# The last quarter of the MLP's down projections computed as seven half-size block products, with some additions done by accumulating DMAs

## The chip, the cores and the metric

The kernel runs on one core of a Trainium2 chip. The metric is the device time of one execution in microseconds (us); lower is better. A core has a matrix engine (TensorE, PE in the profile), three elementwise engines (VectorE or DVE, ScalarE or ACT, GpSimd or POOL), a queue engine that issues transfers (SyncE or SP) and 16 DMA engines. Each engine works through its own instructions in order and waits on semaphores for the others. POOL can issue transfers too, and those may add to what stands at their destination ("accumulating").

## What is computed

Two decoder layers on 512 tokens of width 1024, all in float32. The part that matters here is the MLP of each layer and what follows it:

```python
for i in range(DEPTH):                       # DEPTH = 2
    ...                                      # attention, added to h
    hn = rmsnorm(h, norm_mlp_g[i])
    u = jnp.square(jax.nn.relu(hn @ w_mlp_up[i]))      # 512 x 4096
    h = h + u @ w_mlp_down[i]                          # 512 x 1024
    gate = jax.nn.sigmoid(rmsnorm(h, norm_ple_g[i]) @ w_ple_gate[i])
    h = h + (p[i] @ w_ple_proj[i]) * gate
return rmsnorm(h, final_norm_g)
```

## The kernel before

Activations are held transposed: `h` is eight tiles h0 to h7 of 128 features by 512 tokens. For float32 accuracy each operand is split into a rounded high part and a low part (`hi`/`lo`, `wh`/`wl`, `uh`/`ul`), and each product is three matmuls: high by high, high by low, low by high (`mm3`, L137 to L142). ACT makes the high part with a copy, DVE (in the MLP) the low part with a subtraction, so every piece of weights passes ACT, then DVE, then PE.

The MLP's 4096 hidden features are worked in four chunks `ch` of 1024, each of four blocks `c`. `up(ch, c)` multiplies a block of 256 hidden features into two PSUM banks, and DVE and ACT apply the relu, the scale and the square (L720, L721); L732 and L733 split the result into `uh` and `ul`. `down(ch, c)` multiplies the chunk's hidden features by the weights of output columns 256c to 256c+255, that is h[2c] and h[2c+1].

For the first three chunks, `down` uses a Strassen-Winograd scheme: the product of 2 x 2 blocks from seven block products instead of eight. `up` makes four combinations of the hidden blocks (T1 to T4, L724 to L728), so its split covers 1792 columns; `down` makes four weight sums on DVE (L742 to L745) and takes seven products of 12 matmuls with 256 columns each. Two products go straight into `h` (L784, L786); the four side products are gathered over the chunks in `sides[c]` (L771), and `side_sums(c)`, eight DVE operations on 256 columns, adds them to `h` at the end.

The last chunk (ch = 3) is done in the ordinary way: `down_last(c)` runs 2 x 24 matmuls of 512 columns, DVE adds each bank to `h` (L804), and `nxt.done(k)` prepares the next norm: ACT scales and splits h[k] (L182), DVE makes the low part (L183), ACT squares h[k] (L241), and DVE adds the squares up (L247). Its `up` needs no T blocks and splits 1024 columns.

The order of instructions on each engine is set when the kernel is built, by a scheduler that goes by its own estimate of times; the program text gives dependences and a starting order. Weights come in 1 MB transfers on SP's queue into two buffers named `raw`; the hidden tile `u` and the tile `sums` have one buffer each. In both layers the last chunk is followed by the gate projection, which needs h0 to h7; in layer 1 (`ple_final`) PE first transposes `h` (L858).

Of the kernel before, what the change touches and what calls it, by code (L numbers as in the profile page):

```python
# [12 lines left out]
F32 = mybir.dt.float32  # L13
# [6 lines left out]
P = 128  # L20
D = 1024
S = 512
# [40 lines left out]
def trunk(  # L63
# [8 lines left out]
    def nm(s):  # L72
        uid[0] += 1
        return f"{s}_{uid[0]}"
# [155 lines left out]
    class Norm:  # L230
# [3 lines left out]
        def done(self, k, stats=True):  # L234
            self.hl[k] = split_tile(h[k], gcol(self.kind, self.layer, k))
            if stats:
                self.stats(k)

        def stats(self, k, after=()):
            sq = t2k("e" if self.acc else "rstd")  # L240
            act = nc.scalar.activation(sq, h[k], AF.Square)  # L241
# [460 lines left out]
    def mlp(layer, fpool, norm, nxt):  # L702
# [6 lines left out]
        def up(ch, c):  # L709
# [12 lines left out]
            parts = slice(0, 7)  # L722
            if ch < NCH - 1:
                nc.vector.tensor_tensor(  # L724
                    u[:, T1:T3 + 1:2], u[:, B11:B22 + 1:3], u[:, T3:T3 + 1].to_broadcast([P, 2, HW]), op=ALU.subtract)
                nc.vector.scalar_tensor_tensor(
                    u[:, T2], u[:, T1], -1.0, u[:, B22], op0=ALU.mult, op1=ALU.subtract)
                nc.vector.scalar_tensor_tensor(  # L728
                    u[:, T4], u[:, T2], -1.0, u[:, B21], op0=ALU.mult, op1=ALU.subtract)
            else:  # L730
                parts = slice(B11, B22 + 1)
            nc.scalar.activation(uh[:, parts], u[:, parts], AF.Copy)  # L732
            nc.vector.tensor_tensor(ul[:, parts], u[:, parts], uh[:, parts].bitcast(F32), op=ALU.subtract)  # L733
            hidden[ch, c] = (uh, ul)

        def down(ch, c):
            raw = wload(w_down[layer, 4 * ch + c])
            rv = raw.rearrange("p (s k c) -> p s (k c)", s=4, k=4)
            A12, A22, S3, A11 = range(4)
            sums = fpool.tile([P, 3, S], F32, tag="sums", name=nm("sums"), bufs=1)  # L740
            S1, S2, S4 = range(3)
            nc.vector.tensor_tensor(sums[:, S1], rv[:, S3], rv[:, A22], op=ALU.add)  # L742
            nc.vector.tensor_tensor(sums[:, S2], sums[:, S1], rv[:, A11], op=ALU.add)
            nc.vector.tensor_tensor(rv[:, S3], rv[:, S3], rv[:, A11], op=ALU.add)
            nc.vector.tensor_tensor(sums[:, S4], sums[:, S2], rv[:, A12], op=ALU.add)  # L745

            def split(src):
                n = src.shape[1]
# [4 lines left out]
                src = src.rearrange("p s (k c) -> p s k c", k=4)  # L753
                nc.scalar.activation(hi, src, AF.Copy)  # L754
                nc.vector.tensor_tensor(lo, src, hi.bitcast(F32), op=ALU.subtract)
                return hi, lo
# [9 lines left out]

            def total(x, bank):
                if ch == 0:
                    nc.scalar.activation(sides[c][x], banks[bank], AF.Copy)
                else:  # L770
                    nc.vector.tensor_tensor(sides[c][x], sides[c][x], banks[bank], op=ALU.add)  # L771

            w = split(sums[:, S1:S2 + 1])
# [10 lines left out]
            nc.vector.tensor_tensor(h[2 * c], h[2 * c], banks[2], op=ALU.add)  # L784
            product(3, 0, w, 1, T4, True, True)
            nc.vector.tensor_tensor(h[2 * c + 1][:, 0:HW], h[2 * c + 1][:, 0:HW], banks[3][:, 0:HW], op=ALU.subtract)  # L786
# [10 lines left out]
        def down_last(c):  # L797
            blk = block(w_down[layer, 4 * (NCH - 1) + c], KT, P)
            uhl = [tuple(x[:, B11 + 2 * i:B11 + 2 * i + 2].rearrange("p a c -> p (a c)") for x in hidden[NCH - 1, k])
                   for k in range(4) for i in range(2)]  # L800
            for i in range(2):
                acc = ps_wide()
                lin(acc, blk[i][0], blk[i][1], uhl, 0, KT)
                nc.vector.tensor_tensor(h[2 * c + i], h[2 * c + i], acc, op=ALU.add)  # L804
                nxt.done(2 * c + i)

        for c in range(4):
            up(0, c)
        for ch in range(1, NCH):
            up(ch, 0)  # L810
            for c in range(4):
                down(ch - 1, c)
            for c in range(1, 4):
                up(ch, c)
                if ch == NCH - 1:
                    side_sums(c)
        side_sums(0)
        for c in range(4):
            down_last(c)
# [145 lines left out]
def _feeds(a):  # L965
# [3 lines left out]
    for layer, w in enumerate((a["w_in_even"][0], a["w_in_odd"][0])):  # L969
        blocks = []  # L970
        for j, g in enumerate(GROUPS[layer]):
# [4 lines left out]
            else:  # L976
# [20 lines left out]
        "w_down": np.array([[_pack(down[l], range(8 * ch, 8 * ch + 8), 256 * c, 256, 2) if ch == 3 else  # L997
                             _pack4(down[l], 8 * ch, 256 * c) for ch in range(4) for c in range(4)] for l in layers]),
# [31 lines left out]
```

## Time and profile before

| What | us |
|---|---|
| Median of three timed runs | 1310.36 (1309.34 to 1310.42) |
| The profiled execution, its time | 1308.87 |
| Its span, from first to last instruction | 1307.1 |
| Matmul records busy | 1283.7 |
| VectorE busy | 973.5 |
| ScalarE busy | 686.0 |
| GpSimd busy | 189.8 |

The profile is of one execution of 1308.87 us; 1.8 us of it lie outside the span. Busy times of different engines overlap, so they don't add up to the span. PE has matmul records in 98% of the span; a record's end is modelled and reaches over the start of the next one, so what a matmul costs is read from the distance between starts. GpSimd's busy time lies in the attention parts, where it makes low parts of weights.

### The profile page before, as it was taken

The page shows a single profiled execution, that of the slowest core. Times are in us where ns is not written, and L with a number is a line of the kernel's source. Part 1 is how long each engine was busy: PE and PEld are TensorE (multiplying, and loading weights), DVE is VectorE, ACT ScalarE, POOL GpSimd, SP SyncE. Part 2 cuts the span into 40 slices and gives each one's busy share as a digit, 9 for nine tenths or more (in the row PEclk, how much of TensorE's full clock was granted, in tenths as well). Part 3 has the DMA queues.
Part 4 walks back from the last instruction along what each step waited for, and adds up shares of the span by engine and source line. Part 5 has one row for each costly group of instructions (what it writes and reads, how often), then busy time and mean ns, then how long its engine had stood idle before and what let it go on. Part 6 is the DMA issues. An engine that isn't in the chain of part 4 may idle for free.

```text
span 1307.1 us, 18561 instructions
## 1 busy us (share of the span) xinstructions
PE 1283.7 (98%) x7256; PEld 1117.4 (85%) x7256; DVE 973.5 (74%) x1623; ACT 686.0 (52%) x1117; POOL 189.8 (15%) x160
## 2 busy tenths in 40 slices
PE   9999999999999999999999999999999999999997
PEld 7988787888998989988889888788899898998876
DVE  7788888778848869845767877887784885994566
ACT  6666768554535334333456666765553443533344
POOL 2433434410000000000024333222000000000001
PEclk9999999999999999999999999999999999999999
DMA  6421423223232322323432222212223123232241
GB/s 217 135 81 50 140 93 115 89 82 112 86 108 97 102 92 97 129 97 101 157 112 96 84 89 78 69 57 95 99 97 124 70 97 129 73 122 97 97 145 65
DMA packets 28040, 133.20 MB, mean 102 GB/s; under 512 B 3312, under 2 KB 4048, under 8 KB 15280
## 3 DMA queue, kind: packets, MB, share of 16 engines
q1 hardware_dynamic: 27952, 132.01, 29.5%
q8 instruction: 57, 0.93, 0.3%
q14 instruction: 31, 0.25, 0.1%
HBM read 125.63 MB, written 6.37 MB: 101 GB/s over the span
## 4 chain that ended last, share of the span: by engine, by line
PE 85%; DVE 8%; ACT 4%; issue 1%; DMA 1%; SPq 0%; POOL 0%; ACTq 0%; DVEq 0%; POOLq 0%
PE mm L138 10%; PE mm L141 10%; PE mm L142 10%; PE sc L141 6%; PE sc L142 6%; PE sc L138 6%; PE pv L142 5%; PE pv L141 5%; PE pv L138 5%; PE tp L141 5%; PE tp L142 5%; PE tp L138 5%; PE pv L551 2%; PE tp L532 2%; PE sc L506 1%
## 5 line engine op out<-in xcount | busy, mean ns | idle before, releaser
L122 ACT ACTIVATE wh<-raw 128x1024 fp32r<-128x1024 f32 (+1 forms) x168 | 173.4, 1036 | 226.9 <-PE mm L141 63.0
L126 POOL TENSOR_TENSOR wl<-raw,wh 128x512 fp32r<-128x512 f32 (+1 forms) x132 | 177.1, 1364 | 309.3 <-ACT wh L122 303.6
L138 PE MATMUL mm<-hi,wh 128*128 128x512 f32 x472 | 187.0, 396 | 0.6 <-DVE v L443 0.4
L142 PE MATMUL mm<-hi,wl 128*128 128x512 f32 x472 | 184.8, 392 | 0.1
L141 PE MATMUL mm<-lo,wh 128*128 128x512 f32 x472 | 184.6, 391 | 0.0
L128 DVE TENSOR_TENSOR wl<-raw,wh 128x1024 fp32r<-128x1024 f32 x102 | 124.5, 1224 | 41.3 <-ACT wh L122 34.8
L142 PEld LDWEIGHTS mm<-hi,wl 128*128 128x128 f32 x472 | 88.6, 188 | 20.1 <-POOL wl L126 0.5
L138 PEld LDWEIGHTS mm<-hi,wh 128*128 128x128 f32 x472 | 88.7, 188 | 17.3 <-DVE v L443 0.6
L141 PEld LDWEIGHTS mm<-lo,wh 128*128 128x128 f32 x472 | 88.7, 188 | 15.6
L526 ACT ACTIVATE e<-e,mn 128x128 f32<-128x128 f32 (+3 forms) x96 | 53.8, 561 | 65.4 <-DVE mn L523 65.0
L754 ACT ACTIVATE wh<-raw 128x1024 fp32r<-128x1024 f32 x48 | 50.7, 1057 | 69.6 <-PE tp L141 35.1
L733 DVE TENSOR_TENSOR ul<-u,uh 128x1792 fp32r<-128x1792 f32 (+1 forms) x32 | 58.4, 1824 | 23.4 <-ACT uh L732 23.4
L732 ACT ACTIVATE uh<-u 128x1792 fp32r<-128x1792 f32 (+1 forms) x32 | 49.4, 1544 | 48.9 <-DVE u L728 48.7
L138 PE MATMUL sc<-hi,wh 128*128 128x512 f32 x184 | 71.9, 391 | 0.9 <-ACT hi L182 0.9
L141 PE MATMUL sc<-lo,wh 128*128 128x512 f32 x184 | 72.1, 392 | 0.3 <-DVE lo L183 0.3
L142 PE MATMUL sc<-hi,wl 128*128 128x512 f32 x184 | 71.8, 390 | 0.0
L721 ACT ACTIVATE u<-u 128x512 f32<-128x512 f32 x64 | 39.4, 625 | 53.8 <-DVE u L720 53.8
L142 PE MATMUL pv<-uh,wl 128*128 128x256 f32 (+1 forms) x224 | 67.4, 301 | 0.0
L142 PE MATMUL sc<-uh,wl 128*128 128x256 f32 (+1 forms) x224 | 67.3, 301 | 0.0
L141 PE MATMUL pv<-ul,wh 128*128 128x256 f32 (+1 forms) x224 | 67.2, 300 | 0.0
L141 PE MATMUL sc<-ul,wh 128*128 128x256 f32 (+1 forms) x224 | 67.2, 300 | 0.0
L138 PE MATMUL pv<-uh,wh 128*128 128x256 f32 (+1 forms) x224 | 66.6, 297 | 0.0
(259 smaller groups left out, 3645.4 us busy)
## 6 DMA issues: line engine op xcount, KB each, us to landing
raw<-in_w_up_dram SPq DMA_DIRECT2D x32, 1024.0 KB, 4.9
raw<-in_w_down_dram SPq DMA_DIRECT2D x32, 1024.0 KB, 4.9
raw<-in_w_in_dram SPq DMA_DIRECT2D x23, 1024.0 KB, 4.9
raw<-in_w_gate_dram SPq DMA_DIRECT2D x8, 1024.0 KB, 5.0
bias<-urow SPq DMA_DIRECT2D x24, 256.0 KB, 3.9
raw<-in_w_outa_dram SPq DMA_DIRECT2D x8, 768.0 KB, 4.2
pj<-pjd SPq DMA_DIRECT2D x16, 256.0 KB, 5.0
h<-in_xT_dram SPq DMA_DIRECT2D x8, 256.0 KB, 5.6
```

The lines of the kernel that those rows point to most:

```text
L122: nc.scalar.activation(hi, src, AF.Copy)
L126: nc.gpsimd.tensor_tensor(lo[:, kx], src[:, kx], hi[:, kx].bitcast(F32), op=ALU.subtract)
L128: nc.vector.tensor_tensor(lo, src, hi.bitcast(F32), op=ALU.subtract)
L138: mm = nc.tensor.matmul(acc, lh, rh, start=start, stop=False)
L141: nc.tensor.matmul(acc, lh, rl, start=False, stop=False)
L142: nc.tensor.matmul(acc, ll, rh, start=False, stop=stop)
L526: nc.scalar.activation(e[:, 0:n], e[:, 0:n], AF.Exp, scale=-1.0, bias=mn, accum_out=s)
L532: nc.tensor.transpose(tp[:, j * P:(j + 1) * P], e[:, j * P:(j + 1) * P], ident)
L721: nc.scalar.activation(ui, ui, AF.Square, scale=0.5)
L732: nc.scalar.activation(uh[:, parts], u[:, parts], AF.Copy)
L733: nc.vector.tensor_tensor(ul[:, parts], u[:, parts], uh[:, parts].bitcast(F32), op=ALU.subtract)
L754: nc.scalar.activation(hi, src, AF.Copy)
```

## The change

The last chunk's down projections use the seven products as well, and part of the additions moves from DVE to accumulating DMAs that POOL issues:

- `up` makes the T blocks for every chunk, and its split always covers 1792 columns.
- `down(3, c)` forms two of its weight sums by DMA: the weights' block S3 is loaded into a tile `s1` (two buffers) by SP, block A22 is accumulated onto it by POOL, and block A11 is accumulated onto S3 in `raw`. DVE still makes two sums.
- For c = 0 to 2 the four PSUM banks are collected by `collect`: ACT copies a bank to a staging tile (tag `u`, one buffer), and POOL issues a DMA that adds it to `sides[c][x]`, h[2c] or h[2c+1].
- `finished(c - 1)`, called in `down(3, c)` for c = 1 to 3, runs `side_sums` and `done` for the two `h` tiles of the column before; the squares are added by accumulating DMAs.
- For c = 3 DVE adds straight from PSUM (`combine`).
- The weights of the last chunk are laid out in HBM as those of the others.

```diff
-        def done(self, k, stats=True):
+        def done(self, k, stats=True, dma=False):
...
+            elif dma:
+                nc.gpsimd.dma_start(self.acc, sq, accum_op=ALU.add)
             else:
                 nc.vector.tensor_tensor(self.acc, self.acc, sq, op=ALU.add)
...
-            parts = slice(0, 7)
-            if ch < NCH - 1:
...
-            nc.scalar.activation(uh[:, parts], u[:, parts], AF.Copy)
+            nc.scalar.activation(uh, u, AF.Copy)
...
+            if last:
+                blocks = [src[:, S * x:S * x + S] for x in range(4)]
+                nc.sync.dma_start(s1[:, 0], blocks[S3])
+                nc.gpsimd.dma_start(s1[:, 0], blocks[A22], accum_op=ALU.add)
+                nc.gpsimd.dma_start(rv[:, S3], blocks[A11], accum_op=ALU.add)
+            else:
+                nc.vector.tensor_tensor(s1[:, 0], rv[:, S3], rv[:, A22], op=ALU.add)
+                nc.vector.tensor_tensor(rv[:, S3], rv[:, S3], rv[:, A11], op=ALU.add)
...
+            if last and c < 3:
+                stage = [fpool.tile([P, 7 * HW], F32, tag="u", name=nm("u"), bufs=1), 0]
+
+            def collect(dst, src, sign=1.0):
+                t = stage[0][:, stage[1]:stage[1] + src.shape[-1]]
+                stage[1] += src.shape[-1]
+                nc.scalar.activation(t, src, AF.Copy, scale=sign)
+                nc.gpsimd.dma_start(dst, t, accum_op=ALU.add)
...
+            if last and c:
+                finished(c - 1)
+            if last and c == 3:
+                combine(c, banks[:2], t2k("e"))
...
+        def combine(c, banks, t):
+            left, right = slice(0, HW), slice(HW, S)
+            (s1t1, s2t2), (s3t3, a11b11) = ((x[:, left], x[:, right]) for x in banks)
+            h11, h12, h21, h22 = (h[2 * c + i][:, x] for i in range(2) for x in (left, right))
+            a, x = t[:, left], t[:, right]
+            nc.scalar.activation(a, a11b11, AF.Copy)
+            for dst, y, z, op in ((h11, h11, a, ALU.add), (x, a, s2t2, ALU.add), (h12, h12, x, ALU.add), (h12, h12, s1t1, ALU.add),
+                                  (x, x, s3t3, ALU.add), (h21, h21, x, ALU.subtract), (x, x, s1t1, ALU.add),
+                                  (h22, h22, x, ALU.subtract)):
+                nc.vector.tensor_tensor(dst, y, z, op=op)
+
+        def finished(c):
+            side_sums(c)
+            for i in range(2):
+                nxt.done(2 * c + i, dma=True)
...
-        def down_last(c):
...
-        side_sums(0)
+        side_sums(3)
         for c in range(4):
-            down_last(c)
+            down(NCH - 1, c)
```

Three places show what stands where now (layer 0; layer 1 has the same rows with other numbers).

On ACT, around the second column (c = 1). Before, a column is four operations for each of its two tiles: a weight split (L122), then the scaled split and the square of the h tile just finished.

```order
L122 ACTIVATE wh_1001_5795<-raw_1000_5793 128x1024
L182 ACTIVATE hi_984_5710<-h1_95,gcols_102 128x512
L241 ACTIVATE e_986_5714<-h1_95 128x512
L122 ACTIVATE wh_1003_5799<-raw_1000_5793 128x1024
L182 ACTIVATE hi_993_5753<-h2_96,gcols_102 128x512
L241 ACTIVATE e_995_5757<-h2_96 128x512
```

Now, from the last copy of column 0 (into the staging tile u_993) to the split of column 1's weight sum S4 (e_1020); u_1009 is column 1's staging tile, in the same memory as u_993.

```order
L784 ACTIVATE u_993_5679<-sc_992_5678 128x256
L765 ACTIVATE wh_1022_5903<-raw_1002_5790 128x1024
L765 ACTIVATE wh_1032_5949<-s1_1026_5938 128x512
L784 ACTIVATE u_1009_5803<-tp_1005_5799 128x512
L182 ACTIVATE hi_1014_5874<-h0_94,gcols_102 128x512
L784 ACTIVATE u_1009_5803<-tp_1006_5800 128x512
L241 ACTIVATE rstd_1016_5878<-h0_94 128x512
L182 ACTIVATE hi_1017_5880<-h1_95,gcols_102 128x512
L241 ACTIVATE e_1019_5884<-h1_95 128x512
L765 ACTIVATE e_1020_5887<-sums_1003_5792 128x512
```

The split of S4 now stands behind a copy into u_1009, which has to wait until all four DMAs of column 0 have read u_993, and behind the operations on h0 and h1.

On POOL, at the same place; side_634, side_635, h0 and h1 are the destinations of column 0's collects, s1_1048 is the weight sum of column 3. Before, POOL has no instruction here.

```order
L747 DMA raw_1024_5935<-in_w_down_dram 128x512
L785 DMA side_634_3068<-u_993_5679 128x512
L785 DMA side_635_3069<-u_993_5679 128x512
L746 DMA s1_1048_6084<-in_w_down_dram 128x512
L785 DMA h0_94<-u_993_5679 128x512
L785 DMA h1_95<-u_993_5679 128x256
L785 DMA side_636_3070<-u_1009_5803 128x512
```

The accumulate for column 3's weights was put between column 0's collects, ahead of those into h0 and h1.

On PE, where the last chunk begins. Before, its first matmuls run through two halves of each of the four hidden blocks, and the newest, uh_972, is met after 18 matmuls (one row in three is shown, the high-by-high one):

```order
L138 MATMUL mm_979_5652<-uh_886_4935,wh_975_5644 128x512
...
L138 MATMUL mm_979_5652<-uh_952_5464,wh_975_5644 128x512
...
L138 MATMUL mm_979_5652<-uh_962_5541,wh_975_5644 128x512
...
L138 MATMUL mm_979_5652<-uh_972_5618,wh_975_5644 128x512
```

Now the three older blocks are run into each of four banks (36 matmuls, the last of which is the first row here), then come four matmuls with the newest, uh_984, and then its low part ul_985:

```order
L142 MATMUL sc_992_5678<-uh_974_5575,wl_1001_5759 128x256
L138 MATMUL mm_989_5675<-uh_984_5647,wh_994_5680 128x256
L138 MATMUL mm_990_5676<-uh_984_5647,wh_996_5712 128x256
L138 MATMUL sc_991_5677<-uh_984_5647,e_998_5742 128x256
L138 MATMUL sc_992_5678<-uh_984_5647,wh_1000_5758 128x256
L141 MATMUL mm_989_5675<-ul_985_5648,wh_994_5680 128x256
```

The newest block is met after 36 matmuls of 256 columns instead of 18 of 512, and its split is 1792 columns wide instead of 1024.

More of the change, by code (lines that the diff above doesn't have):

```diff
@@ L741, in down @@
[L741 to L744, printed above, removed]
+            sums = fpool.tile([P, 2, S], F32, tag="sums", name=nm("sums"), bufs=1)
+            s1 = fpool.tile([P, 1, S], F32, tag="s1", name=nm("s1"), bufs=2)
+            S2, S4 = range(2)
+            last = ch == NCH - 1
@@ L745, in down, with split @@
             nc.vector.tensor_tensor(sums[:, S4], sums[:, S2], rv[:, A12], op=ALU.add)
[L747 to L748 removed]
+            def split(*srcs):
+                n = sum(x.shape[1] for x in srcs)
                 if n == 2:
@@ L769, in total @@
                     nc.scalar.activation(sides[c][x], banks[bank], AF.Copy)
-                else:
+                elif not last:
                     nc.vector.tensor_tensor(sides[c][x], sides[c][x], banks[bank], op=ALU.add)
-            w = split(sums[:, S1:S2 + 1])
+                elif c < 3:
+                    collect(sides[c][x], banks[bank])
+            w = split(s1, sums[:, S2:S2 + 1])
             product(0, 0, w, 0, T1, True, False)
```

62 lines of the change are left out of this document (32 added, 30 removed).

## The prediction

> **What bounds the kernel now.** I read the page's busy times and chain first, then the stretches of the two last chunks, then the rows in them.
>
> ```profile
> span 1307.1 us, 18561 instructions
> PE 1283.7 (98%) x7256; PEld 1117.4 (85%) x7256; DVE 973.5 (74%) x1623; ACT 686.0 (52%) x1117; POOL 189.8 (15%) x160
> PE 85%; DVE 8%; ACT 4%; issue 1%; DMA 1%; SPq 0%; POOL 0%; ACTq 0%; DVEq 0%; POOLq 0%
> ```
>
> PE ends 85% of the chain. The table of stretches shows the last chunk of layer 0, then that of layer 1 (length, then busy time of each engine):
>
> ```profile
> 577.00:623.00 46.00, 46.00 (x200) 37.08 (x199) 25.82 (x32) 18.08 (x25) 0.00 (x0) 1.00 0.33 109
> 1205.00:1250.00 45.00, 44.94 (x200) 35.87 (x198) 23.29 (x32) 16.57 (x24) 0.00 (x0) 1.00 0.25 84
> ```
>
> Here PE has no gap at all and the clock is full, while DVE is busy 25.82 us of 46, ACT 18.08 and POOL not once. So in this place each matmul saved is time saved, as long as weights and hidden blocks go on arriving before PE asks for them. The question is whether they do.
>
> **What the products save.** The rows of PE give the first matmul of column 0 and the first matmul behind that column in a chunk that already has seven products; the rows of DVE give one bank of two neighbouring columns of the last chunk.
>
> ```profile
> 333.31 0.28 PE L138 MATMUL sc<-uh,wh 128*128 128x256 f32 x1
> 343.39 0.28 PE L138 MATMUL pv<-uh,wh 128*128 128x256 f32 x1
> 591.06 0.69 DVE L804 TENSOR_TENSOR h<-h,sc 128x512 f32<-128x512 f32 x1 [2.25 <-PE sc L142]
> 602.26 0.69 DVE L804 TENSOR_TENSOR h<-h,tp 128x512 f32<-128x512 f32 x1 [2.20 <-PE tp L142]
> ```
>
> 84 matmuls of 256 columns take 10.08 us, 0.120 each; 48 of 512 columns take 11.20 us, 0.233 each. So the seventh less of arithmetic is worth 1.12 us a column, not 1.4: for four columns in two layers **-9.0 us**. That is the whole gain, and only if nothing makes PE wait.
>
> **Term A: the newest hidden block.** The end of the last up projection before the change, and prices of the wide form from the chunks that have it:
>
> ```profile
> 574.27 0.69 DVE L720 SCALAR_TENSOR_TENSOR u<-pv,rstd 128x512 f32<-128x512 f32 x1 [3.35 <-PE pv L142]
> 575.01 0.62 ACT L721 ACTIVATE u<-u 128x512 f32<-128x512 f32 x1
> 576.76 1.23 DVE L733 TENSOR_TENSOR ul<-u,uh 128x1024 fp32r<-128x1024 f32 x1 [0.39 <-ACT uh L732]
> L724 DVE TENSOR_TENSOR u<-u 128x512 f32<-128x512 f32 x24 | 16.5, 686 | 1.4 <-ACT u L721 1.4
> L726 DVE SCALAR_TENSOR_TENSOR u<-u x24: 416/424/427, 298.5 to 1121.2; 128x256 f32<-128x256 f32 x24
> L732 ACT ACTIVATE uh<-u 128x1792 fp32r<-128x1792 f32 x24 | 40.9, 1704 | 48.7 <-DVE u L728 48.7
> L733 DVE TENSOR_TENSOR ul<-u,uh 128x1792 fp32r<-128x1792 f32 x24 | 48.6, 2024 | 19.8 <-ACT uh L732 19.8
> ```
>
> Now the low part is ready at 577.99, 3.7 us after 574.27, and 18 x 0.233 = 4.2 us of older work cover it. After the change the chain is L720 0.69, L721 0.62, one weight split that DVE has in between (1.22) up to about 2.1 us, then 0.69, twice 0.42 with 0.1 between dependent steps, 1.70 and 2.02: about 7.5 us from the same point, 7.8 from PE's last up matmul. The cover is 36 + 4 matmuls of 0.120 = 4.8. PE waits **3.0 us in each layer**. In earlier chunks `down` comes one `up` later, which hides this; here nothing is left to put in front.
>
> **Term B: the copies, the DMAs and the split of S4.** The trace has no accumulating DMA and none issued by POOL. The nearest rows:
>
> ```profile
> bias<-urow SPq DMA_DIRECT2D x24, 256.0 KB, 3.9
> h<-in_xT_dram SPq DMA_DIRECT2D x8, 256.0 KB, 5.6
> out_dram<-ht SPq DMA_DIRECT2D x8, 256.0 KB, 2.1
> raw<-in_w_down_dram SPq DMA_DIRECT2D x32, 1024.0 KB, 4.9
> 581.98 0.33 SPq L114 DMA_DIRECT2D raw<-in_w_down_dram  x1
> L126 POOL TENSOR_TENSOR wl<-raw,wh 128x512 fp32r<-128x512 f32 x100 | 140.9, 1430 | 235.1 <-ACT wh L122 229.4 <-PE pv L622 5.7
> L769 ACT ACTIVATE side<-sc x8: 577/580/597, 339.1 to 988.2; 128x512 f32<-128x512 f32 x8
> L182 ACT ACTIVATE hi<-h,gcols 128x512 fp32r<-128x512 f32 x48 | 33.5, 713 | 19.8 <-DVE h L804 8.7 <-DVE h L688 7.6 <-DMA h<-in_xT_dram 3.4
> L241 ACT ACTIVATE e<-h 128x512 f32<-128x512 f32 x42 | 25.4, 617 | 4.3 <-DVE h L845 4.3
> L754 ACT ACTIVATE e<-sums 128x512 fp32r<-128x512 f32 x24 | 15.0, 624 | 3.6 <-DVE sums L745 3.6
> L795 DVE TENSOR_TENSOR h<-h,side 128x256 f32<-128x256 f32 x40 | 16.1, 421 | 0.1
> ```
>
> An issue is bounded by 0.33 us (SP's) and 1.43 us (POOL's own work on a tile of this size); I take the middle, 0.9. From issue to landing the same 256 KB takes 2.1 (a store), 3.9 (a load) or 5.6 us (eight loads queued); I take the load, with POOL's 0.9 in place of SP's 0.33: **4.5 us**, 4.1 for half a tile. An accumulate also reads its destination, which speaks against the lower end. The Trainium skill (DMA: Bandwidth & Descriptors, section "Anatomy of one DMA") fits about 2.0 us plus bytes over 436 GB/s for a DMA issued by GpSimd, an estimate of 2.6 us here; by it the sum below would come to about +12 us instead of +24. The 1 MB loads land in 4.9 us where that fit gives 4.4, so the fit is near for plain transfers, but no run here shows an accumulating one.
>
> Count from the end of column 0's last matmul. SP may load column 3's `s1` only after column 1's split has read the buffer, 2.2 us earlier; it lands 3.8 us later, at +1.6. On POOL that accumulate stands ahead of the collects into h0 and h1, so h1's begins at 1.6 + 2 x 0.9 = +3.4 and lands at +7.5. Until then ACT is stuck at its copy into the staging tile, which has one buffer. Behind it stand seven operations, 0.58 + 0.71 + 0.58 + 0.62 + 0.71 + 0.62 + 0.62 = 4.4 us, some 3.9 since neighbours overlap by 0.08, with 0.5 more for the `side_sums` steps that the operations on h wait for. The split of S4 ends at +12.0. PE has 60 matmuls to run meanwhile (column 1's four side products and half a product of column 2), 7.2 us. It waits **4.8 us**.
>
> **Term C: column 2, and what DVE holds back.** The same chain for column 2: the last copy of column 1 is done at +1.5, POOL is free, h3 lands at +5.6, ACT's 4.0 us follow, 9.7 in all. PE has 48 matmuls (5.8 us) and 1.2 us of the next wait: **2.8 us**. That other wait: DVE's step on column 1's sides stands ahead of the low part of column 2's S2, and the side collect, copied by ACT only after the staging tile is free, lands late; S2 is ready 1.2 us after PE wants it, and the same for column 3: **2.4 us**.
>
> **Term D: the last column.** In layer 0 PE has 19 matmuls of the gate projection to run ahead of column 3's S4, 4.3 us, and waits some **1.2 us**. In layer 1 the transposes need h itself, so there is no such cover: **4.5 us**, and `combine` with its eight dependent steps of 0.42 and two splits, where DVE also has to copy the transposes, makes the end about **0.9 us** longer.
>
> What costs nothing: the T blocks of the other three `up` of the chunk (2.4 us more of ACT and DVE, beside 10.9 us of matmuls), and the sums and `side_sums` that move, since DVE is idle for nearly half this stretch. DVE's saved work is worth nothing for that reason too.
>
> **The sum.** Layer 0: 3.0 + 4.8 + 2.8 + 2.4 + 1.2 = 14.2; layer 1: 3.0 + 4.8 + 2.8 + 2.4 + 4.5 + 0.9 = 18.4. Together 32.6 - 9.0 = +23.6. On the profiled execution's 1308.87 us (span 1307.1 and 1.8 around it; the median of the timed runs is 1.5 us higher) that is **1332 us**.
>
> **Rivals.**
> - *The DMAs land early.* At 2.1 us, the store's row, DMAs no longer set B to D; what is left is the order on ACT and DVE: A 3.0, then about 2.3 and 2.0 for columns 1 and 2, 3.3 and 0.9 in layer 1's end, 18.8 - 9.0 less rounding: +10, about 1319 us. For it: these DMAs have the queue nearly to themselves (DMA share 0.33). Against it: an accumulate reads, adds and writes.
> - *The DMAs land late.* From about 5 us on, each accumulated sum of squares, which waits for the one before it, holds POOL's queue in front of the next collects, and the weight sums are late too. Each further us then costs some 14: at 5.6 us +38, 1347 us; at 6, 1351.
> - *The other side: the waits are covered and the products pay.* The mechanism would be a shorter way from column c's last copy to column c + 1's S4. It decides at 7.2 us, PE's own work in between. Then only A remains, 6.0 - 9.0: about 1306 us, and 1300 if A is covered as well. For it: DVE and ACT are half idle. Against it: from the copies to S4 nine ACT operations follow each other in order, with `side_sums` between, which alone is longer than 7.2 us even with DMAs that cost nothing.
> - *It does not do what it says*: the order of instructions shows 84 narrow matmuls a column in the last chunk, so this has no chance worth a number.
>
> **How the numbers follow.** Forecast (DMAs of 3 to 5.2 us) 0.72; early 0.12; late 0.12; covered 0.04, of which I give 0.01 to a result within 0.2% (about what a measurement of this kernel can tell from no change). All but the last are slower by more than 0.2%: slower 0.96, same 0.01, faster 0.03. The range takes in both ends of the DMA's price, 1317 to 1350; only part of the late case and the covered one lie outside.
>
> **What the profile would show.** PE's rows 0.120 apart in the last chunk (the -9.0); a PE gap near 3 us just behind the last up projection that ends on uh and ul (A); gaps of 2 to 5 us once a column that end on ACT's split of `sums` (B, C, D), with ACT idle before its copy into `u` until a DMA landed; from 3 to 5 us to landing for the accumulates and about 0.9 of POOL for each. I am wrong if PE has no gaps there, or if an accumulate lands in under 2 or over 6 us.

## The result, and the profile after

| What | Before | After |
|---|---|---|
| Median of four timed runs, us | 1309.85 (1308.74 to 1310.42) | 1364.28 (1362.95 to 1365.29) |
| The profiled execution, its time and span, us | 1308.87, 1307.1 | 1365.29, 1363.5 |
| Ratio after / before | | 1.0416, 95% interval 1.0400 to 1.0433 |

The kernel became 54.4 us slower. The forecast was 1332 us, 23.6 above the profiled execution, with a range up to 1350: the direction was right, and the loss more than twice as large.

The page of the changed kernel, first the span and the busy times, then the granted TensorE clock in 40 slices:

```profile
span 1363.5 us, 19508 instructions
PE 1294.8 (95%) x7544; PEld 1143.1 (84%) x7544; DVE 1014.7 (74%) x1705; ACT 719.9 (53%) x1191; POOL 233.3 (17%) x210
PEclk9999999999999999978999999999999999998899
```

PE's share fell from 98% to 95% although it has 288 instructions more, and the clock row has dips it did not have. The table of stretches (length, busy time of PE, PEld, DVE, ACT and POOL, granted clock, DMA share) shows the two last chunks, where before PE had no gap and a clock of 1.00:

```profile
600.00:632.00 32.00, 23.88 (x153) 23.68 (x154) 19.28 (x33) 16.54 (x26) 10.41 (x12) 0.73 0.64 123
1262.00:1280.00 18.00, 13.64 (x93) 13.43 (x93) 10.37 (x18) 8.18 (x14) 4.33 (x6) 0.78 0.73 152
```

PE is busy three quarters of the time and, while busy, has the clock only at 0.73 and 0.78. So there are two losses here, waits and a slow clock. The rows of PE that follow a wait (start, duration, what it works on, and in brackets the idle time and what ended it), first layer 0, then layer 1:

```profile
579.87 0.39 PE L138 MATMUL mm<-uh,wh 128*128 128x256 f32 x1 [1.18 <-ACT uh L730]
581.93 0.39 PE L141 MATMUL mm<-ul,wh 128*128 128x256 f32 x1 [1.32 <-DVE ul L731]
604.29 0.58 PE L138 MATMUL pv<-uh,e 128*128 128x256 f32 x1 [8.12 <-ACT e L765]
621.06 0.58 PE L138 MATMUL sc<-uh,e 128*128 128x256 f32 x1 [3.83 <-ACT e L765]
638.18 0.50 PE L142 MATMUL mm<-hi,wl 128*128 128x512 f32 x1 [2.01 <-DVE wl L128]
654.09 0.50 PE L141 MATMUL mm<-lo,wh 128*128 128x512 f32 x1 [4.24 <-DVE lo L183]
...
1237.82 0.39 PE L141 MATMUL mm<-ul,wh 128*128 128x256 f32 x1 [1.32 <-DVE ul L731]
1261.29 0.58 PE L138 MATMUL pv<-uh,e 128*128 128x256 f32 x1 [9.35 <-ACT e L765]
1277.79 0.58 PE L138 MATMUL sc<-uh,e 128*128 128x256 f32 x1 [4.36 <-ACT e L765]
1295.49 0.58 PE L138 MATMUL pv<-uh,e 128*128 128x256 f32 x1 [6.68 <-ACT e L765]
```

The places are those that the prediction named: the newest hidden block (A), the split of S4 in columns 1, 2 and 3 (B, C, D). The time lost at each is 0.16 us more than the bracket, because a record's end lies that much past the place where the next start would have stood. The second loss is seen between the waits. These are starts in column 1 of layer 0, behind the wait of 8.12 us:

```profile
604.88 0.41 PE L138 MATMUL pv<-uh,wh 128*128 128x256 f32 x1
605.10 0.41 PE L141 MATMUL pv<-ul,wh 128*128 128x256 f32 x1
605.31 0.41 PE L142 MATMUL pv<-uh,wl 128*128 128x256 f32 x1
...
610.47 0.28 PE L142 MATMUL pv<-uh,wl 128*128 128x256 f32 x1
610.59 0.28 PE L138 MATMUL pv<-uh,wh 128*128 128x256 f32 x1
610.71 0.28 PE L141 MATMUL pv<-ul,wh 128*128 128x256 f32 x1
```

For some 6 us the matmuls start 0.213 us apart, then 0.120 again. The granted clock there is 0.50 (604.30 to 610.00 us), and this document calls the time lost "half clock". PE's records have no gaps in it, so a search for waits passes over it.

**A ledger of the two losses.** In the two last chunks and what follows them (540 to 665 us and 1190 us to the end) I added up, for each kernel, the time lost in waits of over 0.3 us, and, between neighbouring matmuls without a wait, what their starts stand further apart than 0.120 us (256 columns) or 0.233 us (512). Before has 2.5 us of waits and 1.6 of half clock, and the products save 9.0; so waits + half clock - 13.1 should be the difference in time:

| Kernel | Waits | Half clock | Sum - 13.1 | Measured against before |
|---|---|---|---|---|
| after (profiled execution) | 49.7 | 17.5 | +54.1 | +55.4 |
| collection by VectorE | 18.9 | 9.3 | +15.1 | +15.2 |
| weight sums by VectorE | 38.9 | 15.1 | +40.9 | +40.1 |
| squares by VectorE | 52.4 | 15.8 | +55.1 | +55.8 |
| column 2's squares by VectorE | 47.4 | 16.3 | +50.6 | +50.3 |
| load after collection | 45.9 | 16.9 | +49.7 | +50.0 |
| finishing later | 41.2 | 12.0 | +40.1 | +39.9 |
| a staging tile per column | 50.2 | 15.6 | +52.7 | +50.0 |
| 268 extra matmuls (32.2 us) | 20.5 | 10.8 | +50.4 | +50.2 |
| 329 extra matmuls (39.5 us) | 13.9 | 4.3 | +44.6 | +43.1 |
| no accumulating DMA | 21.5 | 10.4 | +18.8 | +18.9 |
| splits ahead, GpSimd adds | 16.1 | 10.1 | +13.1 | +15.0 |
| splits ahead, VectorE adds | 14.0 | 11.4 | +12.3 | +12.5 |

(The extra matmuls' time, 0.120 us each, is in the sum of their rows; the first row sets the 1365.29 us of the profiled execution against before's median.) Thirteen kernels agree with it within 3 us, nine of them within 1. So the 9.0 us that the products save is there in all of them, and waits and half clock are the whole loss. The ledger only says where the time went; why PE waited is for the experiments. Each of the experiments below is one timed execution beside one of before on the same chip; since executions of one kernel lie up to 2.3 us apart, differences under 3 us are not read.

### The profile page after: what moved, and what is told of

Its sections match the earlier page's. It is cut to its first block, busy times and chain, and to the rows that moved or that the text cites. A ratio compares the mean times of both kernels' runs of the same rounds, so it can differ in the third digit from the quotient of the medians.

```text
span 1363.5 us, 19508 instructions
## 1 busy us (share of the span) xinstructions
PE 1294.8 (95%) x7544; PEld 1143.1 (84%) x7544; DVE 1014.7 (74%) x1705; ACT 719.9 (53%) x1191; POOL 233.3 (17%) x210
## 5 line engine op out<-in xcount | busy, mean ns | idle before, releaser
L122 ACT ACTIVATE wh<-raw 128x1024 fp32r<-128x1024 f32 (+1 forms) x152 | 156.4, 1033 | 162.5 <-PE mm L141 44.4
L128 DVE TENSOR_TENSOR wl<-raw,wh 128x1024 fp32r<-128x1024 f32 x86 | 104.8, 1223 | 32.2 <-ACT wh L122 32.2
L765 ACT ACTIVATE wh<-raw 128x1024 fp32r<-128x1024 f32 x64 | 67.7, 1057 | 67.0 <-PE tp L141 34.9
L746 POOL DMA_DIRECT2D s<-in_w_down_dram x8 | 7.4, 921 | 526.4 <-DVE s L749 506.2
L766 DVE TENSOR_TENSOR wl<-raw,wh 128x1024 fp32r<-128x1024 f32 x64 | 78.2, 1223 | 24.0 <-ACT wh L765 24.0
L731 DVE TENSOR_TENSOR ul<-u,uh 128x1792 fp32r<-128x1792 f32 x32 | 64.8, 2024 | 25.9 <-ACT uh L730 25.9
L730 ACT ACTIVATE uh<-u 128x1792 fp32r<-128x1792 f32 x32 | 54.5, 1703 | 55.3 <-DVE u L728 55.3
L142 PE MATMUL pv<-uh,wl 128*128 128x256 f32 x224 | 64.7, 289 | 0.0
L141 PE MATMUL pv<-ul,wh 128*128 128x256 f32 x224 | 64.6, 289 | 0.0
L142 PE MATMUL sc<-uh,wl 128*128 128x256 f32 x224 | 64.6, 289 | 0.0
```

The costliest lines, as they stand in the source:

```text
L141: nc.tensor.matmul(acc, lh, rl, start=False, stop=False)
L142: nc.tensor.matmul(acc, ll, rh, start=False, stop=stop)
L730: nc.scalar.activation(uh, u, AF.Copy)
L731: nc.vector.tensor_tensor(ul, u, uh.bitcast(F32), op=ALU.subtract)
L765: nc.scalar.activation(hi[:, y], x, AF.Copy)
L766: nc.vector.tensor_tensor(lo[:, y], x, hi[:, y].bitcast(F32), op=ALU.subtract)
```

## Experiments

**Collection.** The banks of columns 0 to 2 are added by VectorE again:

```diff
-                elif not last:
+                elif not (last and c == 3):
                     nc.vector.tensor_tensor(sides[c][x], sides[c][x], banks[bank], op=ALU.add)
-                elif c < 3:
-                    collect(sides[c][x], banks[bank])
...
-            if last and c < 3:
-                collect(h[2 * c], banks[2])
-            else:
-                nc.vector.tensor_tensor(h[2 * c], h[2 * c], banks[2], op=ALU.add)
+            nc.vector.tensor_tensor(h[2 * c], h[2 * c], banks[2], op=ALU.add)
```

> The weight sums and the squares of the last chunk stay on accumulating DMAs; the banks of columns 0 to 2 are added into the side sums and hidden-state tiles by VectorE again, so no staging copy and no collecting DMA is left. Theory (the loss is ScalarE and VectorE standing behind the collecting DMAs, and the half clock that follows TensorE's long waits): no wait over 3.4 us is left before column 1's or column 2's third product, the granted clock stays at 1.00 through the last chunk, and the time is 1316 to 1324 us. Rival, that the weight sums' DMAs are what is late: the time stays above 1350. Rival, that narrow 256-column products do not pay even without waits: 1324 to 1335 with no wait over 1.5 us.

Measured: 1324.87 us, 15.2 over before. PE's rows at the third product of column 1 in layer 0 and of column 3 in layer 1:

```profile
597.12 0.39 PE L138 MATMUL pv<-uh,e 128*128 128x256 f32 x1 [1.27 <-ACT e L765]
1255.51 0.39 PE L138 MATMUL pv<-uh,e 128*128 128x256 f32 x1 [2.04 <-ACT e L765]
```

The long waits are gone, and 39 of the 54 us with them. The clock was not at 1.00 throughout, though: 9.3 us of half clock are left, behind A's two short waits and behind waits of 1 and 2 us. Collection is the main loss; the time came 0.9 us above the theory's range for that remainder. By its time alone the run would fit the rival of narrow products, but that asked for no wait over 1.5 us, and column 3 in layer 1 waits 2.04; the ledger has the products' gain in full.

**Weight sums.** VectorE forms the two sums in the last chunk too:

```diff
-            if last:
+            if False:
                 blocks = [src[:, S * x:S * x + S] for x in range(4)]
```

> Only the weight sums go back to VectorE; collection and squares stay on accumulating DMAs. Theory: the collecting DMAs still hold ScalarE and VectorE, so at least half of the loss stays: 1340 to 1362 us, with waits of 3 us and more before products of the last chunk. Rival, that the weight sums' accumulating DMAs are what is late: 1325 us or less.

Measured: 1349.73 us. As the theory had it, most of the loss stays, but 14.6 us went, though no wait of PE had ended on one of these DMAs. What they did is shown by the next run's rows.

**The load beside the collection.** Column 3's weights are loaded only when column 0's collection has landed:

```diff
-            raw = wload(src)
+            raw = wload(src, landed.get(c, ()) if ch == NCH - 1 else ())
...
-                nc.gpsimd.dma_start(dst, t, accum_op=ALU.add)
+                ad = nc.gpsimd.dma_start(dst, t, accum_op=ALU.add)
+                if c == 0:
+                    landed[3] = [ad.ins]
```

> Nothing is computed differently: the 1 MB load of column 3's down weights waits until the last collecting DMA of column 0 (the 128x256 one) has landed. Theory (that DMA takes 9 to 10 us because the load shares the DMA engines with it): it lands 3.5 to 5 us after its issue, the wait before column 1's third product falls from 8.3 and 9.5 us to 4.5 to 6 us, and the time falls by 5 to 10 us to 1354 to 1359. Rival, that an accumulating DMA behind two others on GpSimd is slow by itself: 9 to 10 us to landing as before, and 1362 us or more.

Measured: 1359.68 us, 0.7 above the theory's range; the waits fell to 5.99 and 6.05 us. First the place after, in the timeline of ScalarE, GpSimd and SyncE's queue:

```profile
591.77 0.63 ACT L765 ACTIVATE wh<-s 128x512 fp32r<-128x512 f32 x1 [1.18 <-PE tp L141]
600.21 0.60 ACT L784 ACTIVATE u<-tp 128x512 f32<-128x512 f32 x1 [7.80 <-DMA h<-u]
603.62 0.61 ACT L765 ACTIVATE e<-sums 128x512 fp32r<-128x512 f32 x1
590.19 2.16 POOL L785 DMA_DIRECT2D h<-u  x2
591.88 0.33 SPq L114 DMA_DIRECT2D raw<-in_w_down_dram  x1
```

ScalarE stands at its copy into the staging tile from 592.4 to 600.2, until the collection into h1 lands; the split of S4 (603.62) stands behind it. While GpSimd still issues h1's DMA, the second of the two, SyncE issues 1 MB of weights. Now the DMA issues between 583 and 603 us (queue, count, size, us from issue to landing), after:

```profile
raw<-in_w_down_dram SPq DMA_DIRECT2D x1, 1024.0 KB, 7.7
h<-u POOLq DMA_DIRECT2D x1, 256.0 KB, 5.8
h<-u POOLq DMA_DIRECT2D x1, 128.0 KB, 9.3
```

with the load held back:

```profile
h<-u POOLq DMA_DIRECT2D x1, 256.0 KB, 5.8
h<-u POOLq DMA_DIRECT2D x1, 128.0 KB, 7.2
```

and with the load, but without the weight sums' DMAs (the run above):

```profile
h<-u POOLq DMA_DIRECT2D x1, 256.0 KB, 4.1
h<-u POOLq DMA_DIRECT2D x1, 128.0 KB, 5.0
```

The same 128 KB take 9.3, 7.2 and 5.0 us (9.9, 6.4 and 5.7 in layer 1). So the landing is late because of what else moves, and it takes both: in the third case the load was there too. The DMA packets by queue show why the two causes can't be given separate shares in layer 0. After, h1's packets start only near 597.5 us: from 595.6 to 597.4 SyncE's queue moves 83 packets and GpSimd's a single one, though the load was issued later than h1's DMA, and from 597.6 to 599.9 GpSimd's queue moves 143. Without the weight sums' DMAs ahead of it, h1 is nearly done when the load's packets begin: 138 packets of GpSimd's queue against 15 of SyncE's from 593.0 to 594.4. So the weight sums' DMA pushes h1 back until the load comes in, and then h1 stands behind the load as well. The expected 3.5 to 5 us were not reached by moving the load alone. The Trainium skill (Trainium Kernel Development and Optimization, section "Key Constraints") says that transfers issued from SyncE, ScalarE and GpSimd run on the same 16 DMA engines and interleave. The packets agree in layer 1, where both queues are served at once (56 packets of SyncE's and 50 of GpSimd's from 1251 to 1253 us); in layer 0 one went nearly behind the other.

**The order of the split.** `finished(c - 1)` is written behind the products of columns 1 and 2 instead of ahead of their third product:

```diff
-            if last and c:
+            if last and c == 3:
                 finished(c - 1)
...
+            if last and 0 < c < 3:
+                finished(c - 1)
```

> The same operations in another order: the finishing steps of columns 0 and 1 (sums of the sides, split and square of the two hidden-state tiles) are written behind the products of columns 1 and 2 instead of ahead of their third product, so the split of S4 no longer stands behind operations that wait for collecting DMAs. Theory: the wait before column 1's third product falls from 8.3 and 9.5 us to under 3.5, column 2's stays under 4, and with less half clock the time is 1336 to 1350 us. Rival, that the collecting DMAs delay the split in another way (through the one staging tile or the DMA engines): 1357 us or more, with waits of over 6 us at the same places.

Measured: 1350.47 us, 0.5 above the theory's range. The rows of PE with its longest waits: column 2's first product, then in layer 0 the gate's weights, which PE takes up ahead of column 3's third product, and in layer 1 that product:

```profile
602.14 0.58 PE L142 MATMUL mm<-uh,wl 128*128 128x256 f32 x1 [3.71 <-DVE wl L766]
632.39 0.80 PE L142 MATMUL mm<-hi,wl 128*128 128x512 f32 x1 [9.39 <-DVE wl L128]
1281.07 0.58 PE L138 MATMUL pv<-uh,e 128*128 128x256 f32 x1 [11.08 <-ACT e L765]
```

The waits ahead of the third product of columns 1 and 2 are gone, which shows that the order caused them. The work that was put off waits in column 3 instead, so 14 us are won and not all.

**The staging tile.** Columns 1 and 2 stage in buffers of their own:

```diff
-                stage = [fpool.tile([P, 7 * HW], F32, tag="u", name=nm("u"), bufs=1), 0]
+                stage = [(fpool.tile([P, 7 * HW], F32, tag="u", name=nm("u"), bufs=1) if c == 0 else
+                          fpool.tile([P, 7 * HW], F32R, tag=("ul", "uh")[c - 1], name=nm("u"), bufs=5).bitcast(F32)), 0]
```

> Each of columns 0 to 2 has a staging tile of its own (columns 1 and 2 take free buffers of the hidden blocks), so ScalarE's copy never waits for the DMAs of the column before. Theory: the operations on the hidden-state tiles, which wait for the same DMAs, still stand ahead of the split of S4, so the wait before column 1's third product stays at 7 us or more and the time at 1358 to 1368 us. Rival, that the one staging tile is what holds ScalarE: 1345 us or less.

Measured: 1360.56 us. The rows of ScalarE at the same place:

```profile
591.25 0.58 ACT L785 ACTIVATE u<-tp 128x512 f32<-128x512 f32 x1
602.57 0.72 ACT L182 ACTIVATE hi<-h,gcols 128x512 fp32r<-128x512 f32 x1 [10.75 <-DVE h L848]
```

The copy goes at once; ScalarE then waits 10.75 us for h itself, ahead of the same split. One engine's order had two reasons to wait for one landing, and taking one away left the other; 4 us were won.

**Squares.** First all of them go back to VectorE, then column 2's alone:

```diff
-                nxt.done(2 * c + i, dma=True)
+                nxt.done(2 * c + i)
```

```diff
-                nxt.done(2 * c + i, dma=True)
+                nxt.done(2 * c + i, dma=c < 2)
```

> Only the squares of columns 0 to 2 go back to VectorE. Theory: these DMAs cost only at the end of layer 0, where VectorE's addition of the seventh square waits for them with the last split queued behind it (a 4.4 us wait of TensorE, with 1.6 us of half clock behind it), so 1356 to 1361 us, with the waits in columns 1 and 2 as before. Rival, that the squares' serial DMAs hold GpSimd's queue and so delay collections: 1345 us or less, with column 2's wait gone.

> Only column 2's two squares go back to VectorE; those of columns 0 and 1, the collection and the weight sums stay on accumulating DMAs. Theory (at the end of layer 0 VectorE's addition of the seventh square waits for column 2's two serial DMAs, with the last split queued behind it, while the other squares' DMAs save VectorE time ahead of columns 1 and 2): the 4.4 us wait and its 1.6 us of half clock at the end of layer 0 go, the waits in columns 1 and 2 stay as they are, and the time is 1357 to 1361 us. Rival, that VectorE is short of time in column 3 as well and gives the gain back there: 1363 to 1367 us, with a longer wait before column 3's third product or at the gate's first matmuls.

Measured: 1365.47 us, 4.5 above the theory's range, and 1360.34, inside it. What the DMAs of the squares do in the changed kernel is seen at the end of layer 0, in the timeline of GpSimd and VectorE (L247 is the DMA, L249 VectorE's addition of a square):

```profile
637.76 0.86 POOL L247 DMA_DIRECT2D rstd<-e  x1 [7.00 <-ACT e L241]
645.74 0.86 POOL L247 DMA_DIRECT2D rstd<-e  x1 [7.11 <-ACT wh L122]
652.68 0.69 DVE L249 TENSOR_TENSOR rstd<-rstd,e 128x512 f32<-128x512 f32 x1 [5.37 <-DMA rstd<-e]
653.29 0.74 DVE L183 SCALAR_TENSOR_TENSOR lo<-h,gcols,hi 128x512 fp32r<-128x512 f32 x1
```

Two DMAs onto one tile follow each other at 8 us (they land 7.4 and 6.8 us after their issue), VectorE's addition waits for both, and the last split, which PE needs at 654.09, stands behind it. In both runs this wait and its half clock are gone. With all squares on VectorE the time didn't fall, because column 2's waits went from 3.98 and 4.53 us to 6.45 and 6.66. Not the additions made them longer but a landing: h3's collect, 128 KB, landed 6.4 and 6.5 us after its issue instead of 3.9 and 4.3, beside a 1 MB load of gate weights, and in layer 0 PE starts again 3.9 us after ScalarE's copy, which waits for that landing, in both runs (617.16 to 621.06 after, 620.05 to 623.96 here). With column 2's squares alone these waits stayed at 4.35 and 4.15, and 4 us were won, although column 1's wait in layer 0 came out at 10.6 us instead of 8.3 (9.0 instead of 9.5 in layer 1). There the DMAs into h0 and h1 both took 10.5 us to landing (5.8 and 9.3 in the changed kernel), with the load of column 3's weights issued 0.2 us behind h1's DMA instead of 1.2. No run varies that distance alone, so that it is the cause is likely and not shown.

**Half clock.** Matmuls whose results are overwritten are put where PE waits for S4 (68, 32; 78, 36, 54), in a second run as many as fit (92, 45; 88, 50, 54):

```diff
+            for n in range(FILL[layer][c] if last else 0):
+                uh, ul = us[n % 4]
+                nc.tensor.matmul(banks[2][:, HW:S], w[0][:, 0, n % 4], uh[:, B11], start=True, stop=True)
             product(2, 1, w4, 0, B22, True, False)
```

> Extra matmuls are added whose results are overwritten: 68 and 32 ahead of the third product of columns 1 and 2 in layer 0, 78, 36 and 54 of columns 1 to 3 in layer 1, 256 columns wide, about 32 us of work for TensorE in places where it waited. Theory (half clock follows a long wait and costs some 16 us): the granted clock stays at 1.00 behind those places, matmuls there are 0.120 us apart and not 0.213, and the time falls to 1350 to 1359 us although TensorE does more. Rival, that the lower clock is not from the waits or costs nothing: matmuls still 0.213 apart, and 1364 us or more.

> The overwritten extra matmuls again, now as many as fit the whole waits: 92 and 45 ahead of the third product of columns 1 and 2 in layer 0, 88, 50 and 54 of columns 1 to 3 in layer 1, some 39 us of work. Theory (each wait, also a short one, is followed by up to 3 us of half clock): the waits at these places are under 0.7 us, the matmuls behind them 0.120 us apart, the time lost to half clock falls from 10.8 us in the run with fewer to 3 to 6, and the time is 1351 to 1357 us. Rival, that half clock there has another cause: 1360 us or more.

Measured: 1360.79 us, then 1353.37. The first missed its range by 1.8 us: it left five waits of 1.4 to 3.1 us at these places and the end of layer 0, and four of them had 1.7 to 3.0 us of half clock behind them, as much as long ones. In the second, column 1 of layer 0 looks so, with the last six extra matmuls in the first row:

```profile
603.78 0.87 PE L811 MATMUL pv<-uh,wh 128*128 128x256 f32 x6
605.04 0.39 PE L138 MATMUL pv<-uh,e 128*128 128x256 f32 x1 [0.40 <-ACT e L766]
...
606.11 0.28 PE L141 MATMUL pv<-ul,e 128*128 128x256 f32 x1
606.23 0.29 PE L142 MATMUL pv<-uh,e 128*128 128x256 f32 x1
```

Starts are 0.120 us apart within 1 us of the place. With 39.5 us more work for PE the kernel is 11 us faster, and half clock fell from 17.5 to 4.3 us: the long waits caused it. Some 3 us of this fall are not the extra matmuls' doing, for they are the half clock behind A's waits, which the edit leaves as they were (1.35 and 1.48 us) and behind which there was none in this run.

The clock records explain that. In the last chunks of every trace that has half clock there the granted clock falls to 0.50, and rises again, only at points that lie whole multiples of 3.41 us apart (in the changed kernel it falls at 582.9, 600.0, 620.5 and 654.6 us). Here are the stretch of 3.41 us that holds most of A's two waits in layer 1 and the one behind it (length, busy time of PE, PEld, DVE, ACT and POOL, granted clock, DMA share), first after, then with 329 extra matmuls:

```profile
1234.87:1238.29 3.42, 1.21 (x8) 1.01 (x9) 2.02 (x1) 0.84 (x1) 0.43 (x1) 1.00 0.51 216
1238.29:1241.70 3.41, 3.41 (x19) 3.41 (x18) 0.40 (x1) 1.06 (x3) 0.43 (x1) 0.50 0.47 77
...
1226.74:1230.15 3.41, 1.91 (x13) 1.71 (x14) 2.02 (x1) 0.13 (x1) 0.86 (x1) 1.00 0.26 108
1230.15:1233.56 3.41, 3.41 (x31) 3.41 (x30) 1.38 (x2) 2.67 (x5) 0.86 (x1) 1.00 0.54 97
```

The same two waits leave PE busy for 1.21 us of one stretch of the grid, or are shared out between two and leave it busy for 1.91. Over all fourteen traces up to the last matmul, every stretch of the grid at full clock in which PE was busy for less than 0.47 of it was followed by half clock, none in which it was busy for more than 0.58, and between these both occur. So whether a wait of 1 to 3 us brings half clock depends on how much of one such stretch it fills, and so on where it falls: of the twenty times that A's pair of waits occurs in ten of the kernels, fifteen had half clock behind them.

**No accumulating DMA at all.** The edits of collection, of weight sums and of all squares together:

```diff
-            if last:
+            if False:
                 blocks = [src[:, S * x:S * x + S] for x in range(4)]
...
-                elif c < 3:
-                    collect(sides[c][x], banks[bank])
...
-                nxt.done(2 * c + i, dma=True)
+                nxt.done(2 * c + i)
```

> Seven products in the last chunk, with weight sums, bank collection and squares all back on VectorE, so no accumulating DMA is left. Theory: VectorE's added work makes it late by 1 to 4 us a column but nothing waits on a DMA; waits of 22 to 25 us in all with up to 9 of half clock: 1324 to 1333 us, close to the run without collecting DMAs. Rival, that VectorE becomes the bound without the DMAs: 1340 us or more. Rival, that the products pay once the DMAs are gone: 1310 us or less.

Measured: 1329.20 us, in the theory's range: 35 us of the 54 go with the DMAs. Beside the run without collection (1324.87) the weight sums and squares on DMAs are worth 4 us together once nothing waits on the collection.

**A version to beat both.** Seven products without accumulating DMAs; each column's sums and splits are written one column ahead, `combine` adds from PSUM in all columns onto sides summed earlier, and block 3 of the hidden features is multiplied last in column 0 (A's cover). The core of it:

```diff
+                if c == 0:
+                    for p in plan:
+                        product(p, range(3), False)
...
+                nw.append(nxw[2]())
+                combine(c, banks[:2])
+                product(plan[5], ks, 0)
```

In the first variant GpSimd makes two weight sums, the additions of squares and three steps of `combine`; in the second VectorE makes them all:

```diff
-            nc.gpsimd.tensor_tensor(h21, h21, y, op=ALU.subtract)
+            nc.vector.tensor_tensor(h21, h21, y, op=ALU.subtract)
```

> Seven products in the last chunk too, but without any accumulating DMA: each column's weight sums and splits are written one column ahead, the banks are combined straight from PSUM on top of sides that were summed earlier, GpSimd adds two of the four weight sums, the squares and three of the eight combining steps, and the newest hidden block is multiplied last over all of column 0's products. Theory: with nothing ahead of the splits TensorE's only waits left are about 1.2 us in each layer for the newest hidden block and some 2 us more at the end of layer 1, so 9.0 us of products less about 5: 1304 to 1309 us, the clock at 1.00. Rival, that narrow products or the added work on VectorE do not pay at all: 1312 us or more.

> The version that writes the splits one column ahead, with GpSimd's additions all given to VectorE. Theory (in the version with GpSimd the two engines held each other up: VectorE's steps with two operands from the on-chip buffer took 1.2 to 2.2 us where they otherwise take 0.4 to 1.2): these steps take 0.42 and 0.7 us, VectorE is busy 14 to 15 us a column, and the time is 1316 to 1324 us, below the 1325.6 of the version with GpSimd in spite of the work added to VectorE. Rival, that its lateness was VectorE's own amount of work: 1328 us or more.

Measured: 1325.62 and 1322.79 us. Neither beats before; the first missed its forecast by 17 us. VectorE's groups in the first (busy time, mean ns of one):

```profile
L795 DVE TENSOR_TENSOR h<-h,e 128x256 f32<-128x256 f32 x8 | 9.0, 1124 | 0.1
L810 DVE TENSOR_TENSOR sums<-sums,raw 128x512 f32<-128x512 f32 x8 | 9.6, 1199 | 0.1
L794 DVE TENSOR_TENSOR e<-e,mm 128x256 f32<-128x256 f32 x4 | 1.6, 410 | 0.0
```

and in the second, with two rows of its timeline:

```profile
L795 DVE TENSOR_TENSOR h<-h,e 128x256 f32<-128x256 f32 x8 | 3.3, 417 | 0.0
L810 DVE TENSOR_TENSOR sums<-sums,raw 128x512 f32<-128x512 f32 x8 | 5.5, 689 | 0.2
...
599.12 0.42 DVE L793 TENSOR_TENSOR h<-h,e 128x256 f32<-128x256 f32 x1
612.33 0.42 DVE L793 TENSOR_TENSOR h<-h,e 128x256 f32<-128x256 f32 x1
```

Beside GpSimd's work the same steps took 1124 and 1199 ns instead of 417 and 689, so the help gained nothing: the two times are 2.8 us apart, too near to be told apart. Without it VectorE comes round once in 13.2 us a column and is busy for 12.72 of them (14 to 15 were expected), where PE needs 10.08 for seven products and 11.20 for the ordinary form: VectorE then sets the column's time, and this version can't have what the products save. ScalarE is busy for 6.12 us of the same 13.21; no run moved some of VectorE's work there.

## Why the prediction was wrong

- **The products, -9.0: right.** The ledger closes with it in every kernel. (Seven products for eight are an eighth less arithmetic, not "the seventh less"; the 1.4 named there is that eighth.)
- **Term A, 3.0 a layer: right** (1.34 + 1.48 = 2.8 in layer 0), but 1.5 us of half clock followed it in each layer of this kernel.
- **The price of a DMA, 0.9 of GpSimd and 4.5 us to landing: right on the mean and wrong where it counted.** GpSimd was held 0.86 to 1.05 us on the mean of each line, and the median landing was 3.5 us for the collection into sides and 4.6 for the squares. The step that failed is in term B: h1's DMA "begins at 1.6 + 2 x 0.9 = +3.4 and lands at +7.5". PE's column 1 starts at 588.8 (604.29, less 8.28 of wait and 60 matmuls of 0.120); from there the DMA was issued at about +2 and landed 9.3 us later, and ScalarE's copy starts at +11.4 (600.21). From there to the end of the split (604.23) it took 4.0 us where 4.5 was said. So order and ScalarE's part were right; the landing, 4.1 us in the forecast, was priced as if the DMA were alone, while the weight sums' DMAs and the 1 MB load kept the engines busy. B was 8.3 and 9.5 us instead of 4.8, C 4.0 and 4.5 instead of 2.8, and column 3 in layer 1 6.8 instead of 4.5.
- **Term D in layer 0, 1.2: wrong.** It was 7.2 (0.7 + 2.2 + 4.4, rounded). The serial squares were seen only in the rival of late DMAs, as something that holds GpSimd; that VectorE's own addition of a square waits for them, with the last split behind it, was left out. That wait is the 4.4, and it goes when column 2's squares go back to VectorE.
- **The waits for S2, 2.4 a layer: did not come.** While S4 is late, S2 has time; they appear as waits of about 1 us in the runs in which S4 is not (606.7 and 608.1 without collection). Terms of one chain were added as if each came in full.
- **The clock: no term at all.** The waits came to 47.2 us over before against 32.6 forecast, 14.6 more; half clock added 15.9. These two are the miss of 31 us (54.4 against 23.6), in about equal parts. The second was to be had from the first, since waits of 3 to 5 us were forecast. The Trainium skill (TensorE: Matmul & The Clock Gate, "Part 1: The HAM clock gate") states that the clock falls to half after an idle window of about 3.4 us and comes back after a busy one as long; by that rule at least B would have been followed by half clock. The trace agrees on the half rate (a granted clock of 0.50) and on stretches of this size, not on a stretch that is idle throughout: two waits of 1.3 and 1.5 us, 2 us apart, had it too, one of 2.8 us (layer 1, load after collection) had not, and the stretches counted above put the limit near half of a stretch busy.

The rival "DMAs late" was right that the DMAs land late, and its time at 6 us, 1351, is still 13 short, for want of the clock. Its reason, that the squares' DMAs hold GpSimd's queue, is not borne out: with the squares on VectorE the waits of columns 1 and 2 did not shrink. "Covered" has no run for it: without a single accumulating DMA 21.5 us of waits remain. What is left open: what the stretches between 0.47 and 0.58 busy go by, why the load's packets went ahead of h1's in layer 0 and beside them in layer 1, and how load and weight sums share h1's late landing.

## What to carry to other kernels

Price a transfer by what else is in flight when it is issued, and look at which instructions stand behind its waiter on the same engine: here one landing that was 4 us late moved ScalarE, VectorE and PE alike, and taking away one of its two waiters won 4 us of 54. When a change makes the matrix engine wait, even 1 to 3 us, reckon with half clock behind the wait, up to 3 us each time here; it came where PE was busy for less than about half of a stretch of 3.41 us. And a scheme with fewer products pays only if the additions it brings fit into one column's time on the engine that makes them.

## What the hardware showed that was not expected

- Half clock can follow short waits: behind 1.35 and 1.48 us (A) 1.5 us were lost, behind 1.4 us in the first run with extra matmuls 1.7, and behind A in the second run with them nothing. It begins on a fixed grid of 3.41 us, when PE was busy for less than about half of the stretch before.
- VectorE's steps on two tiles of the on-chip buffer slow down beside GpSimd's (417 to 1124 ns), steps with one operand in PSUM do not (L794, 410 ns). The Trainium skill (SBUF — State Buffer, section "SBUF: two separate sides") describes a pair of ports that VectorE and GpSimd take exclusively for a whole instruction; the rows agree.
- Two accumulating DMAs onto one tile, with other traffic beside them, followed each other at 8 us.
- A DMA issued earlier can move later: after, h1's 128 KB, issued about 1 us before a 1 MB load, began to move near 597.5 us, when the load's packets were nearly through.
